# Conditioning products of a two-layer diffusion step: their four partial strips go over DRAM and are added by VectorE instead of by a selector matmul

## The chip, the cores and the metric

The kernel runs on one core of one Trainium2 chip. The core has TensorE (PE; its weight loads are shown apart as PEld), VectorE (DVE), ScalarE (ACT), GpSimd (POOL) and SyncE (SP), which here only issues DMAs, and 16 DMA engines. The metric is the device time of one execution in microseconds: the median was 1292.72 us over three runs (1290.27 to 1293.17).

## What is computed

A batch of 256 context tokens and 1024 latent tokens, each a row of 1024 numbers, goes through two layers. Cut to what matters here, with l = 0 the gated linear attention (GLA) and l = 1 the softmax attention:

```python
for l in range(2):
    mod_p = silu(c_ctx) @ w_ada[l] + b_ada[l]      # context tokens, one vector of 3072
    mod_s = silu(c) @ w_ada[l] + b_ada[l]          # latent tokens
    sh, sc, gt = split(mod, 3)                     # shift, scale, gate: 1024 each
    h = rms_norm(x, norm_g[l]) * (1 + sc) + sh
    out = gla_mixer(h) if l == 0 else attention(h)
    x = x + gt * out
```

So there are four conditioning vectors in all, two conditionings by two layers. The shift and scale of layer 0 are needed before any token can be projected; its gate only at layer 0's output projection. The shift and scale of layer 1 are needed when the first finished tile of layer 0 is normalised again, its gate only at the last projection. The weights `w_ada` are 2 x 12 MB, and the products are tiny: two vectors by a matrix.

## The kernel before, in words

All large products are made as three f16 products of a high and a low part, and before each split into parts a weight is scaled by a power of two. `pow2` finds it: VectorE reduces the largest absolute value of each partition, one small matmul against the identity (line 113) spreads the 128 values over a PSUM bank, VectorE reduces that (line 118) and makes the scale in four tiny steps. The bank is named by `p2_bank`: in set-up and in GLA it is "z", a single buffer, which also takes half of the transposes of the tokens in set-up (line 420; the other half take the two "mm" banks).

Set-up loads four tiles of tokens, the first query and key weights and layer 0's shift and scale weights (eight loads of 1 MB), makes silu of the conditioning vectors (`cond_vectors`), normalises and transposes the tokens, splits the weights (`fill`, `split_rank`), and then multiplies the conditioning (`mod_rows`, line 294). Those products are ordered on TensorE behind the maxima of the weights. Then `affine` makes layer 0's scaled shift and scale, and `modulate` applies them to the transposed tokens, with which the first projections (line 557) begin.

The GLA is a loop over 50 slots, one head and one tile of 128 tokens each: four heads by ten tiles for the first scan direction, and each head's second direction one head later. In a slot come the decays, the chunk's own products, the value and gate projections for the next slot (`value_gate`), the scans, and a `filler` that brings in other work: in odd slots up to 31 the load of a block of 256 columns of `w_ada` (`ada_load`; layer 0's four gate blocks first, then layer 1's twelve), in even slots the products of the block loaded before (`gemv`), in the slot after it their sum (`mod_sum`). Other jobs, appended to a list, run in the next slot: splits of the attention weights that go to DRAM for later, output weights, and at slots 34 and 35 layer 1's `affine` and the transposition of its result to rows (`affine_rows`).

`gemv` packs eight small products into four strips of 32 partitions, so that the result in the PSUM bank "mm" is four partial sums, of which two rows in each strip are of use. ScalarE copies it to the tile "mod" (one buffer). `mod_sum` adds the strips with a selector matrix `k.sel` (a one in row 32j+i, column i): for a shift or scale block two matmuls with the copied product as weights (line 335) give the sums transposed, and VectorE adds the bias (line 337); for a gate block one matmul with the selector as weights (line 345) gives rows, VectorE adds the bias loaded for it (lines 344 and 346), and SP stores the rows to `gt_d` in DRAM (line 347). These gate rows use the single buffer "s0" of the scan's start states.

The gate projection's result is copied to the tile "gx" (line 589, two buffers), goes through silu and is multiplied with the normalised scan output (line 748), from where SP stores it (line 749, `og_d<-gx`).

The order of the instructions on each engine is not the order of the code. A planner of the framework simulates the program with modelled times and lets each engine take, of what is ready, what has the best priority; priority follows the order of the code, shifted by the offsets of the table `LATER` for the named blocks (`with self.later(...)`). `issue_after` adds a fixed order on one engine. SP, like each engine, works off its queue in order: a DMA that waits holds up those behind it. A tile of a pool with one buffer is given to its next user when all that read it are done.

Of the kernel before, what the change touches and what calls it, by code (L numbers as in the profile page):

```python
# [17 lines left out]
P = 128  # L18
# [54 lines left out]
class K:  # L73
# [57 lines left out]
    def mulcol(self, a, b, pool, tag, const=None):  # L131
        o = self.t(pool, [P, 1], F32, tag)
# [53 lines left out]
    def fill_out(self, w, st):  # L186
# [13 lines left out]
        so = self.t(self.small, [P, 2], F32, "wso")  # L200
# [69 lines left out]
    def cond_vectors(self, rows, brow):  # L270
        nc, cp = self.nc, self.const
        ps = self.bank("z")
        nc.tensor.transpose(ps[:, 0:32], rows, self.ident[0:32, 0:32])
        nc.tensor.transpose(ps[:, 32:80], brow, self.ident[0:48, 0:48])
        cT = self.t(cp, [P, 80], F32, "cT")
        nc.vector.tensor_copy(cT, ps[:, 0:80])
        self.gT = cT[:, 16:32]
        self.bT = cT[:, 32:80]
        c = self.t(cp, [P, 16], F32, "silu_c")
# [4 lines left out]
        nc.vector.tensor_copy(self.cst[:, :, 0:2], c.rearrange("p (i k) -> p k i", i=2))  # L284
        self.modT = [self.t(cp, [P, 16, 2], F32, f"modT{l}") for l in range(2)]

    def mod_rows(self, rows):
# [12 lines left out]
        for b in range(4):  # L302
            nc.tensor.transpose(ps[:, b * P : b * P + P], m[:, b * P : b * P + P], self.ident)
        nc.vector.tensor_tensor(
            self.modT[0].rearrange("p (j b) i -> p j b i", j=4),
            ps.rearrange("p (b j r) -> p j b r", b=4, j=4)[:, :, :, 0:2],
            self.bT[:, 0:16].rearrange("p (j b) -> p j b", j=4).unsqueeze(3).to_broadcast([P, 4, 4, 2]), ALU.add,
# [7 lines left out]
    def gemv(self, l, b, to):  # L315
# [10 lines left out]
        return l, b, m  # L326


    def mod_sum(self, l, b, m):
        nc = self.nc  # L330
        ps = self.bank("mm")
        if b < 8:
            for j in range(2):
                o = 2 * j
                nc.tensor.matmul(ps[:, o : o + 2], m[:, j * P : j * P + P], self.sel[:, 0:2], start=True, stop=True)
            f = 2 * b
            nc.vector.tensor_tensor(
                self.modT[l][:, f : f + 2, :], ps[:, 0:4].rearrange("p (f i) -> p f i", i=2),
                self.bT[:, 24 * l + f : 24 * l + f + 2].unsqueeze(2).to_broadcast([P, 2, 2]), ALU.add,
            )  # L340
        else:
            a = 256 * (b - 8)
            r = self.t(self.ew, [P, DV], F32, "s0", bufs=1)[0:2, :]
            nc.sync.dma_start(r, self.I["b_ada"][l : l + 1, 2 * D + a : 2 * D + a + 256].to_broadcast([2, 256]))
            nc.tensor.matmul(ps[0:2, 0:256], self.sel[:, 0:2], m, start=True, stop=True)
            nc.vector.tensor_tensor(r, ps[0:2, 0:256], r, ALU.add)  # L346
            nc.sync.dma_start(self.gt_d[l, :, a : a + 256], r)


    def affine(self, l):  # L350
        nc, sp = self.nc, self.const
        mod = self.modT[l]
        gb = self.t(sp, [P, 2, 2, KT], F32, f"gb{l}")
        g, sh = (gb[:, j].rearrange("p i k -> p k i") for j in range(2))
        gT = self.gT[:, 8 * l : 8 * l + 8].unsqueeze(2).to_broadcast([P, KT, 2])
        nc.vector.scalar_tensor_tensor(g, mod[:, 8:16, :], 1.0, gT, ALU.add, ALU.mult)
        m = self.t(self.small, [P, 2], F32, "wmx")
        for j, t in enumerate((mod[:, 0:8, :], g)):
            nc.vector.tensor_reduce(m[:, j : j + 1], t, AX.XY, ALU.max, apply_absolute_value=True)
        mx = self.t(self.small, [P, 1], F32, "af_m", bufs=1)  # L360
        nc.vector.scalar_tensor_tensor(mx, m[:, 1:2], 32.0, m[:, 0:1], ALU.mult, ALU.add)
        s, inv = self.pow2(mx)
        nc.vector.tensor_scalar(sh, mod[:, 0:8, :], s, None, ALU.mult)
        nc.vector.tensor_scalar(g, g, s, None, ALU.mult)
        c = self.t(sp, [P, 1], F32, f"invh{l}")
        nc.vector.tensor_copy(c, inv)
        return gb, g, sh, c


    def affine_rows(self, gb):  # L370
        ps = self.bank("mm")[0:32, 0:P]
        self.nc.tensor.transpose(ps, gb.rearrange("p s i k -> p (s i k)"), self.ident)
        r = self.t(self.ew, [P, 256], F32, "mod", bufs=1)[0:32, 0:P]
        self.nc.vector.tensor_copy(r, ps)
        self.nc.sync.dma_start(self.gb_d.rearrange("s i (k p) -> (s i k) p", p=P), r)
# [30 lines left out]
    def normalise(self, xs, junk):  # L406
        nc = self.nc
        n = len(xs)
        ssq = self.t(self.sm, [P, n], F32, f"nt_s{n}")
# [79 lines left out]
    def rank_scales(self):  # L489
        nc, inv = self.nc, self.inv_rank  # L490
        inv_r = self.mulcol(self.inv_h, inv[:, 0:1], self.small, "inv_r")
# [3 lines left out]
        one = self.t(self.small, [P, 2], F32, "one")  # L495
# [4 lines left out]
        row = self.mulcol(one[:, 0:1], self.sr, self.small, "one_r")  # L500
        ones = self.r[96:98, :]
        nc.vector.tensor_scalar(ones, ones, row[96:98, :], None, ALU.mult)
        t = self.mulcol(inv_r, one[:, 1:2], self.small, "inv_z")
# [74 lines left out]
    def value_gate(self, h, i, w):  # L578
# [8 lines left out]
        if h > 0:  # L587
            x = self.t(self.ew, [P, DV], F32, "gx")
# [335 lines left out]
    def gla_out(self, wo, early, n0):  # L924
# [3 lines left out]
        self.inv_h = self.mod1[3]  # L928
# [14 lines left out]
        for n in range(n0, NT):  # L943
            i = order[n]
            if n == NT - 1:
                self.query_rest()
                with self.tc.issue_after(self.pe):
                    self.query()
                self.key_tile(order[n - 2], wkv)
                self.query_rest()  # L950
            hT, lT, inv = prep.pop(i)
            x = xs.pop(n)
            last = self.residual(i, lambda k: (hT[:, k, :], lT[:, k, :]), wo, inv, x)
            nc.gpsimd.dma_start(self.x1_d[i], x)
            self.last = last
            with self.tc.issue_after(last):
                if n + 2 in rows:
                    prep[order[n + 2]] = self.out_prep(*rows.pop(n + 2))
# [6 lines left out]
            self.mod_tile(i, x, (t[:, 0], t[:, 1]), self.last)  # L965
            for j in {3: (0,), 4: (1, 2), 5: (3,), 6: (4,), 7: (5,), 8: (6,)}.get(n, ()):
                self.key_tile(order[j], wkv)
            if n == 8:
                with self.tc.issue_after(self.pe):
                    self.query()  # L970
            if n == n0:
# [9 lines left out]
                with self.tc.issue_after(last):  # L981
                    self.att_setup(*ckv)
                    self.key_setup(*ckv, inv)
# [298 lines left out]
    def attention(self, wo, wk):  # L1282
# [7 lines left out]
        for n, (p, c) in enumerate(self.steps):  # L1290
# [8 lines left out]
            for e in range(4):  # L1299
                h = 4 * p + e  # L1300
                if later:
                    self.nc.sync.dma_start(*later.pop(0))
                PT = self.t(self.sp, [P, 20, 256], F16, "PT", bufs=3)
                self.scores(h, c, 0, q[(p, c, 0)], PT)
                if e % 2 == 0:
                    self.query()
                    self.rest()
                    self.scores(h, c, 1, q[(p, c, 1)], PT)
                else:
                    self.query_rest()  # L1310
                if len(pend) == 2:
                    self.values(*pend[0], g.pop(pend.pop(0)[0]))
                else:
                    self.key_tile(len(pend), wkv)
                if e % 2 == 1:
                    self.scores(h, c, 1, q[(p, c, 1)], PT)
                pend.append((h, c, PT))
                if e % 2 == 1:
                    g.update({i: self.gateT(i, c, *wg[p]) for i in (h - 1, h)})
                    self.rest()  # L1320
# [9 lines left out]
        self.out_tile(OUT[0], 0, self.t(self.sp, [P, TS + PAST], F32, "p")[:, 0:D], wo)  # L1330
        for t in pend:
            self.values(*t, g.pop(t[0]))
# [50 lines left out]
def emit(ctx, tc, I, O, dbg=None, stop=None):  # L1383
# [15 lines left out]
    k.gt_d = k.t(k.dram, [2, 2, D], F32, "gt_d")  # L1399
    k.gb_d = k.t(k.dram, [2, 2, D], F32, "gb_d")  # L1400
# [6 lines left out]
    k.sel = k.t(k.const, [P, 2], F32, "sel")  # L1407
# [5 lines left out]
    with ExitStack() as c:  # L1413
# [5 lines left out]
        k.p2_bank = "z"  # L1419
        banks = ("z", "cs", "A", "kt", "U", "o")  # L1420
        k.gla_init()
        with ExitStack() as c1:
# [3 lines left out]
            rows = k.t(k.p1, [32, P], F32, "rows")  # L1426
            brow = k.t(k.p1, [48, P], F32, "brow")
# [3 lines left out]
            small(rows[16:32, :], I["norm_g"].rearrange("l (k p) -> (l k) p", p=P))  # L1431
# [267 lines left out]
```

## Time and profile before

| | before |
|---|---|
| median of three runs | 1292.72 us |
| profiled execution, own time | 1293.64 us |
| its span | 1291.9 us |
| TensorE busy | 1209.2 us, 94% |
| VectorE busy | 920.0 us, 71% |
| ScalarE busy | 706.0 us, 55% |
| granted TensorE clock, mean | 0.991 |

The span is that of one execution as the profiler saw it; its own time is 1.7 us longer. Rows of groups give a line, an engine, an operation, the tile written and those read, the shapes, a count, and times in nanoseconds. Rows of the time line give the start and the length in microseconds; in brackets the idle time before, and what ended it. Matmuls overlap: the next one starts before the last one has ended. An f32 matmul shows as two records. The stages are roughly these: set-up to 85 us, GLA to 560 us, the output projection of layer 0 with the keys and values of layer 1 to 700 us, attention to 1190 us, the last projection to the end.

### The profile page before, as it was taken

Reading aid. Unit: us, or ns where it says so; the run is one execution under the profiler, and the core shown is the slowest. Engines: PE = TensorE matmul, PEld = TensorE weight load, DVE = VectorE, ACT = ScalarE, POOL = GpSimd, SP = SyncE. Lnnn points to the kernel's source line nnn. Section 1 sums busy time; section 2 is a strip of 40 time slices with the busy share of each in tenths; the row PEclk is TensorE's granted clock in tenths of the full one; section 3 lists DMA queues with packets and bytes.
Section 4 is the critical chain, followed back from the end, with each engine's and each line's share of the span. In section 5 each row is a group of like instructions: output and inputs, shape, how many; then the busy total and the mean of one; then the engine's idle time right before and its main releaser. Section 6 shows DMA issues by size and latency. Waiting matters only on the chain. (4 is left out here: it accounts for less than half of the span.)

```text
span 1291.9 us, 22221 instructions
## 1 busy us (share of the span) xinstructions
PE 1209.2 (94%) x7936; PEld 778.7 (60%) x7936; DVE 920.0 (71%) x2120; ACT 706.0 (55%) x1706; POOL 353.3 (27%) x594
## 2 busy tenths in 40 slices
PE   3899999999999989897999889999999999989998
PEld 1367666655555546664776557676666767656444
DVE  4676678877778789767676667677767677785552
ACT  2684466756656656642334376666767686673110
POOL 1132113223321243410223334342243345312000
PEclk9999999999999999998999999999999999999999
DMA  9711566455555543459965696667957657879432
GB/s 358 259 34 34 164 199 202 149 166 159 160 158 177 172 127 107 147 138 329 210 143 156 176 200 121 136 135 131 198 116 164 136 106 145 185 138 228 139 143 82
DMA packets 357454, 207.51 MB, mean 161 GB/s; under 512 B 251054, under 2 KB 341438, under 8 KB 354912
## 3 DMA queue, kind: packets, MB, share of 16 engines
q1 hardware_dynamic: 349824, 188.02, 57.1%
q0 software_dynamic: 4080, 12.73, 3.0%
q10 hardware_dynamic: 3440, 5.35, 1.1%
q8 instruction: 62, 1.02, 0.3%
q14 instruction: 48, 0.39, 0.1%
HBM read 107.45 MB, written 37.26 MB: 112 GB/s over the span
## 5 line engine op out<-in xcount | busy, mean ns | idle before, releaser
L155 PEld LDWEIGHTS <-hT_hi 128*128 128x128 f16 x1920 | 188.8, 99 | 124.2 <-issue 12.4
L155 PE MATMUL mm<-whi,hT_hi 128*128 128x512 f16 (+1 forms) x576 | 201.1, 349 | 2.9 <-ACT gx L589 1.8
L155 PE MATMUL mm<-whi,hT_lo 128*128 128x512 f16 (+1 forms) x576 | 200.8, 349 | 0.2 <-DMA hT_lo<-hl 0.2
L155 PE MATMUL mm<-wlo,hT_hi 128*128 128x512 f16 (+1 forms) x560 | 195.0, 348 | 0.0
L1214 DVE SCALAR_TENSOR_TENSOR phl<-p,srec,phl 128x1280 f16<-128x1280 f32 (+1 forms) x80 | 107.6, 1347 | 72.4 <-POOL phl L1211 37.9
L155 PEld LDWEIGHTS <-whi 128*128 128x128 f16 x1232 | 120.1, 98 | 60.8 <-issue 2.4
L155 PE MATMUL mm<-hT_hi,whi 128*128 128x256 f16 (+1 forms) x480 | 141.0, 294 | 0.7 <-DVE s L346 0.7
L155 PE MATMUL mm<-hT_hi,wlo 128*128 128x256 f16 (+1 forms) x480 | 141.0, 294 | 0.0
L155 PE MATMUL mm<-hT_lo,whi 128*128 128x256 f16 (+1 forms) x480 | 141.0, 294 | 0.0
L155 PEld LDWEIGHTS <-hT_lo 128*128 128x128 f16 x960 | 94.5, 98 | 70.0 <-DMA hT_lo<-k 5.4
L1181 PE MATMUL S<-kT,wst 128*128 128x512 f16 (+1 forms) x624 | 122.9, 340 | 12.7 <-ACT p L1189 12.2
L155 PE MATMUL mm<-PT,vh 128*128 128x256 f16 x672 | 112.2, 273 | 9.8 <-DMA PT<-phl 8.0
L1211 POOL TENSOR_SCALAR phl<-p,srec 128x1280 f16<-128x1280 f32 (+1 forms) x40 | 57.2, 1430 | 192.1 <-DVE srec L1205 83.1
L1184 DVE TENSOR_REDUCE smx<-S 128x1 f32<-128x1280 f32 (+1 forms) x80 | 101.5, 1269 | 9.2 <-PE S L1181 9.0
L1189 ACT ACTIVATE p<-S,snb,sexp 128x1280 f32<-128x1280 f32 (+1 forms) x80 | 99.4, 1242 | 5.3 <-DVE phl L1214 1.8
L1181 PEld LDWEIGHTS <-wst 128*128 128x128 f16 x624 | 61.1, 98 | 65.7 <-issue 14.5
L155 PE MATMUL mm<-PT,vl 128*128 128x256 f16 x336 | 91.6, 273 | 0.0
L155 PEld LDWEIGHTS <-wlo 128*128 128x128 f16 x616 | 60.3, 98 | 31.5 <-DVE wlo L1352 1.8
L155 PEld LDWEIGHTS <-vh 128*128 128x128 f16 x672 | 65.1, 98 | 20.7 <-issue 9.4
L1019 POOL TENSOR_TENSOR rope<-hx,ropet 128x64 f32<-128x64 f32 x160 | 63.1, 424 | 32.2 <-ACT hx L1145 16.7
L178 DVE TENSOR_REDUCE wmx<-wst 128x1 f32<-128x512 f32 x104 | 65.0, 676 | 5.9 <-DMA wst<-in_att_w_in 2.5
L1186 ACT ACTIVATE snb<-smx,nsexp 128x1 f32<-128x1 f32 x80 | 23.3, 291 | 75.3 <-DVE smx L1184 73.4
(370 smaller groups left out, 2694.5 us busy)
## 6 DMA issues: line engine op xcount, KB each, us to landing
wada<-in_w_ada SPq DMA_DIRECT2D x16, 1024.0 KB, 5.2
wst<-in_gla_w_in SPq DMA_DIRECT2D x12, 1024.0 KB, 5.0
wst<-in_att_w_in SPq DMA_DIRECT2D x10, 1024.0 KB, 5.5
og_d<-gx SPq DMA_DIRECT2D x40, 128.0 KB, 2.7
og_d<-og POOLq DMA_DIRECT2D x40, 128.0 KB, 3.0
wst<-og_d SPq DMA_DIRECT2D x5, 1024.0 KB
xr<-x_d SPq DMA_DIRECT2D x9, 512.0 KB, 6.4
out<-xr ACTq DMA_DIRECT2D x17, 256.0 KB, 3.0
```

What stands on the lines that cost most here:

```text
L155: self.pe = self.nc.tensor.matmul(out, a, b, start=k == 0 and j == 0, stop=k == n - 1 and j == 2).ins
L178: nc.vector.tensor_reduce(mx[:, j : j + 1], st[:, 2 * j : 2 * j + 2, :], AX.XY, ALU.max, apply_absolute_value=True)
L1019: nc.gpsimd.tensor_tensor(tv[:, h, :, w, :], xv[:, h, :, 1 - w, :], sn[:, :, w, :], ALU.mult)
L1181: nc.tensor.matmul(S[:, a : a + n], x, y, start=m == 0, stop=m == 2)
L1184: last = nc.vector.tensor_reduce(mx, S, AX.X, ALU.max).ins
L1186: nc.scalar.activation(nb, mx, AF.Copy, scale=self.nsexp)
L1189: nc.scalar.activation(p, S, AF.Exp, scale=self.sexp, bias=nb, accum_out=den)
L1211: nc.gpsimd.tensor_scalar(hi, p, r, 2.0 ** 14, ALU.mult, ALU.mult)
L1214: nc.vector.scalar_tensor_tensor(lo, p, r2, hi, ALU.mult, ALU.subtract)
```

## The change

Layer 0's shift and scale are made as before. The other sixteen blocks keep their products and the copy to "mod", but the copy is now stored to a new DRAM tensor `md_d` of 128 rows by 3072 columns for each layer. `mod_load` brings back what is wanted in a layout with 8 neighbouring columns in each of the 128 partitions, the four strips side by side (runs of 32 bytes): once in slot 9 for layer 0's gate, once in slot 34 for all of layer 1. It reads into the "mod" buffer. A job in slot 11 (`gate_rows`) and one in slot 36 (`mod_rows_out`) add the strips with reductions on VectorE, add the bias, and store the gate to `gt_d`; the second also makes layer 1's scaled shift and scale and stores them to `gb_d` directly in the order of rows. The selector, the second layer's transposed biases and norm weights, `affine_rows` and its transposing matmul are gone. `affine` is split: `fit` is its part common to both layers.

In set-up, `p2_bank` is "o" instead of "z" (again "z" from the end of set-up). The tile "gx" of the GLA has three buffers. Tiles of single columns in the pool "small", and the sums of squares in `normalise`, are given fewer buffers. Many calls in the attention layer and in its approach are wrapped in `later` with new names, for which the table has no entry, so that their offset is 0.

```diff
-    def cond_vectors(self, rows, brow):
+    def cond_vectors(self, rows):
...
-        nc.tensor.transpose(ps[:, 0:32], rows, self.ident[0:32, 0:32])
-        nc.tensor.transpose(ps[:, 32:80], brow, self.ident[0:48, 0:48])
+        nc.tensor.transpose(ps[:, 0:40], rows, self.ident[0:40, 0:40])
...
     def gemv(self, l, b, to):
...
         m = self.t(self.ew, [P, 256], F32, "mod", bufs=1)
         nc.scalar.copy(m, ps[:, 0:256])
-        return l, b, m
-    def mod_sum(self, l, b, m):
...
-                nc.tensor.matmul(ps[:, o : o + 2], m[:, j * P : j * P + P], self.sel[:, 0:2], start=True, stop=True)
...
-            r = self.t(self.ew, [P, DV], F32, "s0", bufs=1)[0:2, :]
-            nc.sync.dma_start(r, self.I["b_ada"][l : l + 1, 2 * D + a : 2 * D + a + 256].to_broadcast([2, 256]))
-            nc.tensor.matmul(ps[0:2, 0:256], self.sel[:, 0:2], m, start=True, stop=True)
-            nc.vector.tensor_tensor(r, ps[0:2, 0:256], r, ALU.add)
-            nc.sync.dma_start(self.gt_d[l, :, a : a + 256], r)
+        nc.sync.dma_start(self.md_d[l, :, 256 * b : 256 * b + 256], m)
+
+    def mod_load(self, l, s, n):
+        t = self.t(self.ew, [P, 256], F32, "mod", bufs=1)
+        md = t[:, 0 : 64 * n].rearrange("p (s j i k) -> p s j i k", s=n, j=4, i=2)
+        bias = t[:, 192 : 192 + 8 * n].rearrange("p (s k) -> p s k", s=n)
+        src = self.md_d[l].rearrange("(j r) (s p k) -> s r p j k", r=32, s=3, k=KT)
+        load = self.nc.sync.dma_start
+        for m in range(n):
+            for i in range(2):
+                load(md[:, m, :, i], src[s + m, i])
+        load(bias, self.I["b_ada"][l].rearrange("(s p k) -> p s k", s=3, k=KT)[:, s : s + n])
+        if n == 3:
+            load(t[:, 216:224], self.I["norm_g"][l].rearrange("(p k) -> p k", k=KT))
+        return l, md, bias, t[:, 216:224]
+
+    def mod_sum(self, md, bias, tag):
+        nc = self.nc
+        n = md.shape[1]
+        m = self.t(self.const, [P, n, 2, KT], F32, tag)
+        for a in range(n):
+            nc.vector.tensor_reduce(m[:, a], md[:, a].rearrange("p j i k -> p i k j"), AX.X, ALU.add)
+        nc.vector.tensor_tensor(m, m, bias.unsqueeze(2).to_broadcast([P, n, 2, KT]), ALU.add)
+        return m
+
+    def gate_store(self, l, m):
+        self.nc.sync.dma_start(self.gt_d[l].rearrange("i (p k) -> p i k", k=KT), m)
+
+    def gate_rows(self, l, md, bias, _):
+        self.gate_store(l, self.mod_sum(md, bias, "gm")[:, 0])
+
+    def mod_rows_out(self, l, md, bias, gn):
+        m = self.mod_sum(md, bias, "mod1")
+        self.gate_store(l, m[:, 2])
+        gb = self.t(self.const, [P, 2, 2, KT], F32, "gb1")
+        c = self.t(self.const, [P, 1], F32, "invh1")
+        s, inv = self.fit(m[:, 0], m[:, 1], gb[:, 0], gn.unsqueeze(1).to_broadcast([P, 2, KT]))
+        self.nc.vector.tensor_scalar(gb[:, 1], m[:, 0], s, None, ALU.mult)
+        self.nc.vector.tensor_scalar(gb[:, 0], gb[:, 0], s, None, ALU.mult)
+        self.nc.vector.tensor_copy(c, inv)
+        for j in range(2):
+            self.nc.sync.dma_start(self.gb_d[j].rearrange("i (p k) -> p i k", k=KT), gb[:, j])
+        self.inv_h1 = c
+
+    def fit(self, sh, sc, g, gn):
+        nc, sp = self.nc, self.small
+        nc.vector.scalar_tensor_tensor(g, sc, 1.0, gn, ALU.add, ALU.mult)
+        m = self.t(sp, [P, 2], F32, "wmx")
+        for j, t in enumerate((sh, g)):
+            nc.vector.tensor_reduce(m[:, j : j + 1], t, AX.XY, ALU.max, apply_absolute_value=True)
+        mx = self.t(sp, [P, 1], F32, "af_m", bufs=1)
+        nc.vector.scalar_tensor_tensor(mx, m[:, 1:2], 32.0, m[:, 0:1], ALU.mult, ALU.add)
+        return self.pow2(mx)
...
-    def affine_rows(self, gb):
-        ps = self.bank("mm")[0:32, 0:P]
-        self.nc.tensor.transpose(ps, gb.rearrange("p s i k -> p (s i k)"), self.ident)
...
-            x = self.t(self.ew, [P, DV], F32, "gx")
+            x = self.t(self.ew, [P, DV], F32, "gx", bufs=3)
...
-        k.p2_bank = "z"
+        k.p2_bank = "o"
...
+        k.p2_bank = "z"
         k.tl = k.pool("tl", ctx=c)
...
         def filler(slot):
             if slot < 4:
                 prompt(slot)
-            if part:
-                k.mod_sum(*part.pop())
+            if slot in (9, 34):
+                gm.append(k.mod_load(*((0, 2, 1) if slot == 9 else (1, 0, 3))))
+            if slot in (10, 35):
+                k.jobs.append(((k.gate_rows if slot == 10 else k.mod_rows_out), *gm.pop()))
             if slot % 2 == 0:
                 if held:
-                    part.append(k.gemv(*held.pop()))
+                    k.gemv(*held.pop())
...
-            if slot == 34:
-                k.jobs.append((lambda: setattr(k, "mod1", k.affine(1)),))
-            if slot == 35:
-                k.jobs.append((k.affine_rows, k.mod1[0]))
...
             if n == NT - 1:
-                self.query_rest()
+                with self.later("x.qr"):
+                    self.query_rest()
...
```

More of the change, by code (lines that the diff above doesn't have):

```diff
@@ L284, in cond_vectors @@
         nc.vector.tensor_copy(self.cst[:, :, 0:2], c.rearrange("p (i k) -> p k i", i=2))
-        self.modT = [self.t(cp, [P, 16, 2], F32, f"modT{l}") for l in range(2)]
+        self.modT = self.t(cp, [P, 16, 2], F32, "modT")
     def mod_rows(self, rows):
@@ L957, in gla_out @@
                 if n + 2 in rows:
-                    prep[order[n + 2]] = self.out_prep(*rows.pop(n + 2))
+                    with self.later("x.prep"):
+                        prep[order[n + 2]] = self.out_prep(*rows.pop(n + 2))
             load(n + 2)
@@ L1633, in _constants @@
     f32 = np.float32
-    sel = np.zeros((P, 2), f32)
-    for j in range(4):
-        for i in range(2):
-            sel[32 * j + i, i] = 1
     half = P // 2
```

148 lines of the change are left out of this document (73 added, 75 removed).

## The prediction

> **What bounds the kernel now.** First the page: its span and engine rows, and the PE row of the 40 slices.
>
> ```profile
> span 1291.9 us, 22221 instructions
> PE 1209.2 (94%) x7936; PEld 778.7 (60%) x7936; DVE 920.0 (71%) x2120; ACT 706.0 (55%) x1706; POOL 353.3 (27%) x594
> PE   3899999999999989897999889999999999989998
> ```
>
> TensorE is busy 94% of the span; the low digits are the first slice (set-up) and the middle. The view of busy time by stretch shows where TensorE has no slack (columns: stretch, PE busy, PEld, DVE, ACT, POOL, clock, DMA share, GB/s).
>
> ```profile
> 107.00:450.00 343.00, 341.65 (x2094) 202.58 (x2092) 263.97 (x714) 200.97 (x517) 86.51 (x155) 1.00 0.53 163
> 450.00:500.00 50.00, 44.10 (x225) 25.96 (x218) 44.58 (x131) 29.30 (x85) 21.19 (x34) 0.94 0.36 108
> 500.00:550.00 50.00, 44.58 (x301) 32.17 (x300) 38.36 (x108) 33.33 (x88) 19.40 (x32) 0.99 0.44 141
> 550.00:600.00 50.00, 45.09 (x315) 30.84 (x313) 32.20 (x79) 17.23 (x35) 7.09 (x13) 0.97 0.78 208
> 600.00:650.00 50.00, 45.59 (x356) 35.11 (x354) 39.23 (x90) 17.85 (x40) 10.54 (x22) 0.97 0.99 234
> ```
>
> From 107 to 450 us TensorE is busy 341.65 of 343 us, VectorE only 263.97. The conditioning products run exactly there, in the odd jobs of slots 2 to 33. A microsecond of TensorE work removed in this stretch is a microsecond of the span, unless VectorE takes over. From 450 to 650 TensorE idles 200 − (44.10 + 44.58 + 45.09 + 45.59) = 20.6 us: there waits decide.
>
> **1. The sums leave TensorE.** The rows of the selector tile and of the copies into the strips, the selector's busy time in the stretch, and four starts on the time line:
>
> ```profile
> L335 PE MATMUL mm<-sel,mod x32: 167/251/251, 201.9 to 367.9; 128*128 128x2 f32 x32
> L345 PE MATMUL mm<-mod,sel x16: 377/378/378, 119.2 to 461.3; 128*2 128x256 f32 x16
> L325 ACT COPY mod<-mm x16: 351/368/389, 110.0 to 452.1; 128x256 f32<-128x256 f32 x16
> 107.00:450.00 343.00, 8.23 (x46) 5.36 (x46) 1.00 0.53 163
> 119.16 0.59 PE L345 MATMUL mm<-mod,sel 128*2 128x256 f32 x2
> 119.69 0.23 PE L629 MATMUL cs<-cum,ghi 128*128 128x130 f16 x1
> 201.91 0.50 PE L335 MATMUL mm<-sel,mod 128*128 128x2 f32 x4
> 202.28 0.68 PE L676 MATMUL U<-v,ks 128*128 128x256 f32 x2
> ```
>
> Four L335 records make one sum of a shift or scale block, two L345 records one of a gate block: eight sums of each kind. Busy time overlaps its neighbours, so I price by starts: 119.69 − 119.16 = 0.53 and 202.28 − 201.91 = 0.37 us. 8 × 0.53 + 8 × 0.37 = 7.2 us; the busy 8.23 us is the other bound. I take −7.2, because the next instruction's start is what moves. The layer-1 transpose of the scaled rows (L372) goes too, in the stretch with idle time: nothing. The 16 products stay, and each still needs its "mm" bank and its copy L325.
>
> **2. The way over DRAM, on the queues.** SP loses 8 bias loads and 8 gate stores and one store of rows; it gains 16 strip stores, 2 strip loads and a bias load with one store (gate of layer 0), and 6 strip loads, bias, norm weight and three stores (layer 1): 31 issues for 17.
>
> ```profile
> L347 SPq DMA_DIRECT2D gt_d<-s x8: 250/264/317, 123.2 to 467.1; - x8
> SPq L347 <- DVE s L346: 22.1, 5, 12.8
> q1 hardware_dynamic: 77324, 62.18, 50.0%
> ```
>
> 14 more issues at 0.26 to 0.32 us are 4 us of a queue that mostly waits, spread over 400 us: nothing. Each strip store makes SP wait for its ScalarE copy; queued behind are the gated-row stores and the weight loads. The old gate stores made SP wait 22.1 us in five cases for the sum, and VectorE never showed it. I take nothing, with +2 as the upper end. The layer-1 loads are 6 × 512 + 384 + 128 = 3,584 pieces of 32 B. From 107 to 512 us, 77,324 packets took 50.0% of 16 engines' 405 us, 42 ns each; 3,584 × 42 / 16 = 9.4 us, an estimate and an upper one, as those packets average 0.8 KB. Their reader runs as a job of slot 36, the loads go out in slot 34; slots last (452.1 − 110.0) / 30 = 11.4 us by the L325 row. The cover is at least one slot, so nothing; with the cover gone VectorE would stand for up to 9.4 us. The Trainium skill, page "DMA: Bandwidth & Descriptors" (Specifications), speaks against this part: it has transfers below 512 B do a read-modify-write, and asks for 512 B or more at line rate. No row here has a load of 32 B pieces, so the trace can't settle it; it is rival D below.
>
> **3. VectorE takes the sums.**
>
> ```profile
> L346 DVE TENSOR_TENSOR s<-mm,s x8: 402/405/412, 122.7 to 466.6; 2x256 f32<-2x256 f32 x8
> L359 DVE TENSOR_REDUCE wmx<-modT x2: 156/160/163, 43.7 to 482.8; 128x1 f32<-128x16 f32 x2
> L473 DVE TENSOR_REDUCE wmx<-wada x1: 406/406/406, 25.2 to 25.2; 128x1 f32<-128x256 f32 x1
> ```
>
> Eight adds of 0.405 us (3.2 us) and eight small adds go, four reductions over 64 elements come, between 0.16 and 0.41 us each by the two reductions shown, and two small adds. VectorE comes out some 2 us lighter, but off the path up to 450 us: nothing. Around 490 us, where it is busy 44.58 of 50, three of the reductions come together ahead of layer 1's maximum: up to +1, as the copy of the transposed rows goes there. I take 0.
>
> **4. The wait it adds.** The strips are read into the single "mod" buffer in slot 9; the reduction that frees it is a job of slot 11; the product of slot 10 wants the same buffer for its copy. So that product sits in one of the two "mm" banks until the job has run, up to one slot (11.4 us). Behind it TensorE has the value and gate projections, which then have one bank and must wait for ScalarE's copies, two per slot. The nearest row for such a wait is TensorE on the gate copy, in part 6: 1.8 us in four cases, about 0.45 each. Two to eight such waits: +1 to +4. I take +1: it happens once, the product is late in its slot.
>
> **5. Set-up's maxima in bank "o".** Rows of PE, VectorE and ScalarE on the time line:
>
> ```profile
> 29.33 1.11 PE L420 MATMUL z<-ident,x 128*128 128x128 f32 x4 [0.79 <-DVE xT L1458]
> 31.23 0.27 PE L113 MATMUL z<-ident,wm 128*128 128x128 bf16 x1 [0.78 <-DVE xT L1458]
> 32.83 1.94 PE L294 MATMUL A<-whi,cst 128*32 128x512 f32 x8
> 40.07 1.89 PE L294 MATMUL A<-hT_lo,cst 128*32 128x512 f32 x16
> 25.49 1.21 DVE L474 TENSOR_REDUCE wmx<-wada 98x1 f32<-98x1024 f32 x1
> 27.50 0.17 DVE L284 COPY cst<-silu_c 128x16 f32<-128x16 f32 x1
> 28.59 0.69 DVE L1458 COPY xT<-z 128x512 f32<-128x512 f32 x1 [0.91 <-PE z L420]
> 30.49 0.69 DVE L1458 COPY xT<-z 128x512 f32<-128x512 f32 x1 [1.21 <-PE z L420]
> 31.53 0.29 DVE L118 TENSOR_REDUCE p2m<-z 128x1 f32<-128x128 f32 x1 [0.35 <-PE z L113]
> 39.55 1.28 DVE L484 SCALAR_TENSOR_TENSOR wa<-wada,p2s,wa 34x1024 f16<-34x1024 f32 x1
> 40.87 1.14 ACT L485 ACTIVATE wa<-wada,p2s 1x1024 f16<-1x1024 f32 x1 [1.86 <-DVE wa L484]
> 42.04 0.37 ACT L299 COPY mod<-A 128x256 f32<-128x256 f32 x1
> ```
>
> The first maximum (L113) queues for bank "z" behind the last transpose, though its weights are ready much earlier; the layer-0 products (L294) are ordered behind the third maximum and run 32.83 to 41.96. With a bank of their own the maxima need only L474 (done 26.70), and the products also L284 (27.67): they could start 5.2 us earlier. But VectorE is nearly full: it ends at 40.83 (L484) and can only reclaim its 0.91 + 1.21 + 0.35 = 2.5 us of idle time. ScalarE's L485 follows L484, and the copy L299, on which the modulation of all tokens hangs, follows L485. So I take −2.5; the ends are −4.9 (the planner puts L299 ahead of L485) and 0 (the full DMA queue delays the last weight rows). Dropping one constant load and two bias rows: nothing, they land before the first transposes need VectorE.
>
> **6. A third gate buffer.** The waits view, 500 to 650 us, and one line from the gate tile's view (ScalarE's idle time, by what ended it):
>
> ```profile
> PE mm L155 <- ACT gx L589: 1.8, 4, 0.6
> PE o L736 <- POOL Sc L701: 1.6, 1, 1.6
> PE z L736 <- POOL Sc L701: 1.4, 1, 1.4
> PE y L155 <- DMA hT_lo<-k: 4.9, 1, 4.9
> PE kv L113 <- DVE amx L1076: 4.1, 1, 4.1
>   DMA og_d<-gx: 6.0, 7
> ```
>
> ScalarE waits 6.0 us for gated rows to leave, and TensorE 1.8 us for ScalarE. I take −1.5 of the 1.8; the upper end adds the 3.0 us of scan waits that a gate projection run ahead could fill: −4.8; the lower end is 0.
>
> **The rest of the edits.** Fewer buffers for one-off columns and sums of squares: the cover is that each is used once or twice; nothing. The named priority blocks have no entry in the offsets table: offset 0, nothing.
>
> **Sum.** −7.2 + 0 + 0 + 1 − 2.5 − 1.5 = −10.2. The profiled execution took 1293.64 us, 0.92 above the median of the runs; 1293.64 − 10.2 − 0.92 = 1282.5 us. With the bounds of the parts alone, 1275 to 1290.
>
> **The rivals.**
> A, the bounds all fall well: −8.2 − 4.9 − 4.8 = −17.9, 1275 us. For it: no row excludes them. Against: three ends at once.
> B, VectorE takes over as pace-maker: it is at 44.58 of 50 us after 450 us and would have to be above TensorE for long stretches before. Only then is half of the 7.2 lost, and with the bank hold (+4) and set-up at 0 the result is 1292.7 − 3.6 − 1.5 + 4 = 1291.6. Against: 263.97 of 343.
> C, slower: the order on the engines is written by a planner from modelled times, and removing 16 sums and adding DRAM round trips makes it write another one for 450 to 650 us, where TensorE's idle 20.6 us are a few long waits (4.9 and 4.1 above): in order, it stands wherever a modelled time was too short. Doubled, they cost 20.6: 1303. It cancels the gain from +10.2, and ends slower from +12.8. For it: such waits exist already. Against: they could as well shrink.
> D, the strips come late: the 32 B pieces cost so much more than 42 ns that the reader on VectorE stands before layer 1's modulation. At twice the estimate, 18.8 us, against one slot of 11.4, VectorE loses 7.4 and TensorE after it: 1290. Its rule is the one named in part 2.
>
> **How the numbers follow.** Main case 0.52 (1283, own range 1277 to 1289); A 0.16; B 0.10; C 0.16; D 0.06. Range 1273 to 1296: below A by 2 for the planner's luck, and into C. 0.2% is 2.6 us, about what a measurement of this kernel can tell: faster means below 1290.1. That holds for the main case, A, and a third of B and D, 0.73; the same 0.10; slower is C and a little of B, 0.17.
>
> **What would show it.** No selector rows on PE, and the products, values and gates of slots 2 to 33 about 7 us shorter at an equally full PE; L294's first row near 28 to 30 us and the first projection (L557) 2 to 3 us ahead of before; TensorE's wait on the gate copies near 0; one held bank around slot 10; VectorE not standing on a DMA before layer 1's shifts and scales. It is wrong if PE's idle time between 450 and 650 us grows by over 10 us, if PE is no longer full up to 450, or if the attention stage, which the edits don't touch, moves by several microseconds.

## The result and the profile after

The changed kernel takes 1285.75 us (1278.49 to 1288.88), before in the same comparison 1292.99 us: a ratio of 0.9933, 95% interval 0.9909 to 0.9958. Two further comparisons gave 0.9906 [0.9886, 0.9927] and 0.9914 [0.9895, 0.9933]. It is faster by 7 to 12 us; forecast were 10.2. The sum came out nearly right, but two of its terms did not: what was booked to the sums on TensorE comes only in the company of the third gate buffer, which was booked at 1.5 us. That the total is near has luck in it.

The page of the changed kernel, span and engines, and the granted clock in 40 slices (the profiled execution took 1285.86 us):

```profile
span 1284.1 us, 22149 instructions
...
PE 1199.3 (93%) x7886; PEld 777.7 (61%) x7886; DVE 916.8 (71%) x2109; ACT 703.1 (55%) x1706; POOL 351.0 (27%) x594
...
PEclk9999999999999999988999999999999999999999
```

50 matmul records fewer, TensorE's busy time 9.9 us lower, VectorE's 3.2. The stretches, with the columns of the prediction's view:

```profile
104.00:439.00 335.00, 332.63 (x2059) 200.56 (x2057) 264.68 (x706) 201.48 (x521) 85.57 (x156) 1.00 0.56 174
...
450.00:650.00 200.00, 181.12 (x1244) 129.61 (x1243) 155.24 (x404) 95.20 (x240) 56.38 (x97) 0.95 0.70 181
```

104 to 439 us is the stretch of the products now. TensorE is still full (332.63 of 335) and VectorE far from it. From 450 to 650 TensorE idles 18.9 us (20.6 before), at a mean clock of 0.95. Set-up, on the time line:

```profile
27.99 1.94 PE L292 MATMUL A<-whi,cst 128*32 128x512 f32 x8
...
38.25 1.06 PE L292 MATMUL A<-hT_lo,cst 128*32 128x512 f32 x8 [1.57 <-DMA hT_lo<-in_w_ada]
...
40.74 0.19 DVE L302 TENSOR_TENSOR modT<-cs,cT 128x32 f32<-128x32 f32 x1 [0.53 <-PE cs L301]
```

The products start at 27.99 instead of 32.83 us, but at 38.25 they stand 1.57 us on a DMA: the last weight rows. The first projection (L569 now) is 2.7 us ahead of before. The strip loads, by their source line:

```profile
L334 SPq DMA_DIRECT2D mod<-md_d x8: 359/500/1861, 177.8 to 449.5; - x8
...
DMA to landing us min/median/max: 2.0/3.9/4.7
```

and the reductions of layer 1 by theirs:

```profile
L345 DVE TENSOR_REDUCE mod<-mod x3: 242/242/246, 479.4 to 479.7; 128x16 f32<-128x64 f32 x3
```

The loads in pieces of 32 bytes land 2.0 to 4.7 us after their issue, against a cover of one slot (11.4 us). Three reductions run at 479.4 us, some 25 us behind their loads. And what TensorE waits for between 440 and 640 us (us in total, times, longest):

```profile
PE kv L113 <- DVE amx L1099: 8.9, 1, 8.9
PE y L155 <- DMA hT_hi<-q: 4.7, 1, 4.7
PE z L748 <- POOL Sc L713: 3.3, 1, 3.3
PE o L748 <- POOL Sc L711: 2.2, 1, 2.2
PE mm L155 <- ACT gx L601: 1.1, 1, 1.1
```

The wait on the gate copies is down from 1.8 to 1.1 us, and the wait for the attention's maxima, `amx`, has grown from 4.1 to 8.9.

**Where the lead comes and goes.** The lead is the start of an instruction before less its start in the changed kernel. It is 2.8 us at the first product copy and 13.1 at the last one, 16.8 at the last product of the scan with its state (537 us before, `o<-Sc,qe`), 19.8 at the first product of layer 0's output (574 us), 15.3 at the first query copy (703 us), 18.0 at 889, 11.4 at 1113, and 8.0 at the end. So TensorE's lead grows to some 20 us, against 10.2 forecast, and more than half of that is lost again. ScalarE's gate copy at 538 us is 26.7 us ahead, but a copy with a third buffer may start sooner without TensorE being sooner. The experiments ask where the lead comes from and who takes it.

### The profile page after: what moved, and what is told of

Read it like the earlier page. It is cut to its first block, busy times and chain, and to the rows that moved or that the text cites. A ratio compares the mean times of both kernels' runs of the same rounds, so it can differ in the third digit from the quotient of the medians.

```text
span 1284.1 us, 22149 instructions
## 1 busy us (share of the span) xinstructions
PE 1199.3 (93%) x7886; PEld 777.7 (61%) x7886; DVE 916.8 (71%) x2109; ACT 703.1 (55%) x1706; POOL 351.0 (27%) x594
## 5 line engine op out<-in xcount | busy, mean ns | idle before, releaser
L1204 PE MATMUL S<-kT,wst 128*128 128x512 f16 (+1 forms) x624 | 122.5, 338 | 12.6 <-ACT p L1212 11.8
```

Of the source, the lines that this page charges most:

```text
L1204: nc.tensor.matmul(S[:, a : a + n], x, y, start=m == 0, stop=m == 2)
```

## The experiments

Theory 1 is the prediction's: a microsecond taken from TensorE in the full stretch is a microsecond of the time, and the parts add up. Theory 2: behind 450 us TensorE stands on waits, and what was gained before is given back there.

**Each part alone.** `e_sums` is the changed kernel with the other two parts undone:

```diff
-            x = self.t(self.ew, [P, DV], F32, "gx", bufs=3)
+            x = self.t(self.ew, [P, DV], F32, "gx")
...
-        k.p2_bank = "o"
+        k.p2_bank = "z"
```

> Only the strips over DRAM, summed by VectorE; maxima in bank z, two gate buffers. Theory 1 (each microsecond of TensorE work taken out of the full stretch is a microsecond of the time): set-up as before, first product copy at 110.0 us; the copies draw ahead slot by slot, the last one at 444 to 446 us (452.1 before), and the total is 5 to 8 us shorter. Theory 2 (the order is written anew and the stalls after 450 us and the half-clock windows that follow them decide): the last product copy is early as by theory 1, but the total lies anywhere from 15 us shorter to 5 longer, with the difference made between 500 and 620 us or in half-clock windows.

`e_bank` is before with "o" for the maxima of set-up, and "z" again ahead of the loop over the slots:

```diff
-        k.p2_bank = "z"
+        k.p2_bank = "o"
...
+        k.p2_bank = "z"
```

> Only the set-up's maxima in bank o. Theory 1: first projection at 44.8 us (47.4 before), first product copy near 107.3, last one near 449.5, total 2 to 3 us shorter. Theory 2: the same 2.6 us up to 110 us, then the total moves by up to 5 us either way, at the stalls after 450 us.

`e_gx` is before with the third buffer and with the smaller column tiles that make room for it:

```diff
...
-            x = self.t(self.ew, [P, DV], F32, "gx")
+            x = self.t(self.ew, [P, DV], F32, "gx", bufs=3)
```

> Only the third gate buffer, with the smaller column buffers that make room for it. Theory 1: no change up to 450 us (copies at 110.0 and 452 us), the wait of TensorE for gate copies between 500 and 560 us falls from 1.8 to under 0.5 us, total 0 to 2 us shorter. Theory 2: the gate projections run ahead through the last ten slots and free more than that, 5 to 10 us by 560 us, of which the output stage gives part back.

`e_again` is the changed kernel itself:

> The changed kernel again, for a second profile. Theory 1: 1283 to 1288 us, the same waits in the same places, the lead over before 13 us at the last product copy, 15 at the first score product, 8 at the end. Theory 2: the places of the instructions are the same, but the half-clock windows fall elsewhere, and with them several of the 18.7 - 10.4 = 8.3 us of lost clock by which its first profile is worse than that of before.

Measured: sums alone 1.0007 [0.9988, 1.0025], bank alone 0.9962 [0.9947, 0.9977], third buffer alone 0.9982 [0.9967, 0.9997], all of it 0.9906. The three ratios multiply to 0.9951; the parts do not add up. Above all, the part with most of the forecast gain brings none alone, though its TensorE is 10.7 us ahead at the last product copy.

**Two parts at a time, and the sums gone without a substitute.** `e_nogx` is the changed kernel with the first edit of `e_sums` only:

> The changed kernel with two gate buffers again: sums and bank without the third buffer. Theory 1 (the parts add up): sums alone measured 1.0007 and the bank alone 0.9962, so 0.997, some 1289 us, and the third buffer is worth what it was alone, 2.3 us in ratio 0.9982. Theory 2 (what is gained before 540 us is given back in the output stage of layer 0, where the DMA queues set the pace, by how the waits fall): the sum of the parts does not hold; anything from 0.993 to 1.000, and TensorE's lead over before at the first score product (10 us or more at 452 us) says how much came through.

`e_bankgx` is before with the edits of `e_bank` and `e_gx`:

> Before with the maxima in bank o and the third gate buffer, the sums still on TensorE. Theory 1: 0.9962 x 0.9982 = 0.9944, some 1286 us; then the sums bring only 0.1 to 0.4 per cent in company. Theory 2: the third buffer's lead is given back at 600 to 620 us as it was when it stood alone, and 0.996 is left, the bank's part, which went through when alone.

`e_nosum` is before without the sums:

```diff
-        ps = self.bank("mm")
+        ps = m
...
-                nc.tensor.matmul(ps[:, o : o + 2], m[:, j * P : j * P + P], self.sel[:, 0:2], start=True, stop=True)
...
-            nc.tensor.matmul(ps[0:2, 0:256], self.sel[:, 0:2], m, start=True, stop=True)
```

> Before with the 48 selector matmuls of the 16 sums left out and nothing put in their place: VectorE adds the bias to the unsummed product, so the conditioning rows of all sums are wrong and the output with them. No strips go over DRAM. Theory 1: TensorE 7.2 to 10 us ahead at 452 us and the same at the end: 0.992 to 0.9945. Theory 2: 7 to 10 us ahead at 452 us, at most 3 us of it left at 700 us, ratio 0.998 to 1.001. If the loss of some 6 us at 955 to 1030 us in the changed kernel comes from the added DMA issues, it is absent here; if it comes from TensorE being ahead, it is here too.

`e_sumsgx` is the changed kernel with `p2_bank` back to "z", and `e_again2` the changed kernel beside it:

> The changed kernel with the set-up's maxima back in bank z: sums and third buffer. Theory 1 (the parts add up): 1.0007 x 0.9982 = 0.9989. Theory 3 (the third buffer is what lets the sums' gain through: with TensorE ahead, ScalarE's gate copies come too late for two buffers): TensorE 20 us or more ahead at 540 us as in the changed kernel, ratio 0.993 to 0.996, only the set-up's 2.6 us or a little more short of the whole change.

> The changed kernel once more, beside the runs below: 0.9906 to 0.9933 as measured before, some 1283 to 1286 us.

All eight combinations, with the ratio to before, the lead in us at four instructions (named by their time before; the last scan product is TensorE's, the copies are ScalarE's), and ScalarE's idle time ahead of the gate copies that ends with the store of an earlier tile's rows, `og_d<-gx`:

| kernel | ratio, 95% interval | last product copy, 452 | gate copy, 538 | last scan product, 537 | first query copy, 703 | ScalarE on `og_d<-gx` |
|---|---|---|---|---|---|---|
| before | 1 | 0 | 0 | 0 | 0 | 6.0 us |
| third buffer | 0.9982 [0.9967, 0.9997] | 0.0 | 4.3 | -2.4 | -0.8 | 1.4 us |
| bank | 0.9962 [0.9947, 0.9977] | 3.6 | 6.0 | 6.2 | 6.5 | 4.9 us |
| bank, third buffer | 0.9988 [0.9971, 1.0004] | 3.2 | 9.1 | 2.4 | 3.8 | 1.4 us |
| sums | 1.0007 [0.9988, 1.0025] | 10.7 | 11.0 | 11.0 | 4.8 | 20.1 us |
| sums, bank | 0.9999 [0.9981, 1.0017] | 12.6 | 13.9 | 14.0 | 5.3 | 23.5 us |
| sums, third buffer | 0.9931 [0.9918, 0.9944] | 11.5 | 25.0 | 16.3 | 13.0 | 4.1 us |
| all | 0.9914 [0.9895, 0.9933] | 14.9 | 27.9 | 18.9 | 18.5 | 4.0 us |

(The rows of the first column name the parts that are in; the last one is `e_again2`. The leads come from one profiled execution each; those of "bank, third buffer" and "all" were the fastest of theirs, 4 and 6 us below the median, so the ratios are the firmer column.) Read the rows with the sums in pairs. TensorE is 11 to 15 us ahead at the last product copy in all four. At the last scan product it is 11 and 14 us ahead with two gate buffers, 16 and 19 with three. The gate copy at 538 us overstates this: with the third buffer alone it starts 4.3 us earlier while TensorE is 2.4 us behind.

With the sums gone the third buffer is worth 0.76% (1.0007 to 0.9931, 9.8 us), and 0.85% with the bank as well. With the sums in place it is worth 0.18%, and with the bank as well it costs 0.26% (0.9962 to 0.9988; `e_bankgx` lies above what either theory gave). The other way round, the sums gone are worth 0.51 and 0.74% where the third buffer is in (6.6 and 9.6 us), and nothing or a loss where it is not. Each of these differences is uncertain by some 3 us. That is Theory 3 of the expectation. Its mechanism begins in the view of the tile gx (ScalarE's idle time by what ended it), here of `e_sums`:

```profile
  DMA og_d<-gx: 20.1, 9
  PE mm L155: 16.0, 24
```

and of the changed kernel:

```profile
  PE mm L155: 21.4, 26
  ACT ls L258: 5.4, 8
  POOL ors L146: 4.2, 8
  DMA og_d<-gx: 4.1, 3
```

Before, the same line had 6.0 us. With TensorE ahead and two buffers it is 20.1 us in nine waits, during which ScalarE does nothing else.

How TensorE comes to pay for it shows in a stretch that `e_sums` and `e_sumsgx` run with the same 268 matmuls in the same order. First the busy times in `e_sums`, then in `e_sumsgx`, then what ScalarE waits for in `e_sums` from 443 to 500 us:

```profile
442.67:498.00 55.33, 52.89 (x268) 31.57 (x268) 46.18 (x132) 30.67 (x87) 19.50 (x34) 0.97 0.43 124
```

```profile
441.53:492.86 51.33, 51.33 (x268) 31.95 (x269) 46.41 (x134) 32.07 (x93) 19.26 (x34) 0.97 0.47 140
```

```profile
ACT gx L601 <- DMA og_d<-gx: 8.5, 2, 5.3
```

`e_sums` needs 55.33 us and `e_sumsgx` 51.33. In `e_sums` ScalarE stands 8.5 us on the stores of earlier rows, in `e_sumsgx` it never does, and TensorE has six short waits of 0.3 to 0.5 us for results of ScalarE and VectorE that `e_sumsgx` has not. They are 2.4 of the 4.0 us; the rest are starts that come late while the matmul before still runs. `e_nogx` and `e_again2` differ by 4.3 us in the same stretch. So some 4 of the 9.8 us are shown as the price of the missing buffer. The rest is not traced to it: from 499 us on the planner gives TensorE another order in some 38 places, and no run holds the order and changes only the buffer.

TensorE's waits in `e_sums`, 440 to 650 us:

```profile
PE y L155 <- DMA hT_hi<-oghl: 12.8, 1, 12.8
PE mm L155 <- ACT gx L601: 4.4, 2, 3.5
PE o L748 <- POOL Sc L711: 2.6, 1, 2.6
PE kv L113 <- DVE amx L1099: 2.2, 1, 2.2
```

and in `e_sumsgx`, 440 to 640 us:

```profile
PE kv L113 <- DVE amx L1099: 9.5, 1, 9.5
PE y L155 <- DMA hT_hi<-q: 5.0, 1, 5.0
...
PE mm L155 <- ACT gx L601: 1.9, 2, 1.4
```

The wait on the gate copies went from 1.8 us before to 4.4, and with the third buffer to 1.9. The long wait of 12.8 us in the output stage is not what the third buffer removes: `e_sumsgx` stands 9.5 and 5.0 us in the same place, where `e_sums` stands 12.8 and 2.2.

`e_nosum` takes 1.0039 [1.0021, 1.0058]: with the work of the sums gone and nothing added, the kernel is slower, which neither theory gave. So the way over DRAM and VectorE's reductions are not what eats the gain in `e_sums` (1.0007); work taken from TensorE alone is worth nothing here. ScalarE stands 12.7 us on `og_d<-gx` in it, but TensorE only 0.4 us on a gate copy; whether a third buffer would bring its gain through was not run. It is 7.8 us ahead at the last product copy, 0.8 at 703 us, 5.7 behind at 1113.

**More work in the same place.** `e_dblsum` doubles the selector matmuls of before; those of the gate blocks are shown:

```diff
...
-            nc.tensor.matmul(ps[0:2, 0:256], self.sel[:, 0:2], m, start=True, stop=True)
+            for _ in range(2):
+                nc.tensor.matmul(ps[0:2, 0:256], self.sel[:, 0:2], m, start=True, stop=True)
```

> Before with every selector matmul of the 16 sums done twice (the second writes the same values over the first). Theory 1 (a microsecond of TensorE work in the full stretch is a microsecond of the time): 7 to 10 us behind at 452 us and at the end, 1.0055 to 1.008. Theory 2 (the output stage of layer 0 is paced by its queues and VectorE): 7 to 10 us behind at 452 us, most of it made up by shorter waits of TensorE between 540 and 650 us, ratio 1.000 to 1.003.

Measured 1.0130 [1.0105, 1.0155], 16 us: more than either theory gave. Its profiled execution, at 1319.44 us, is the slowest of six and 9 us above their median, so the losses read from it are on the large side. TensorE is 9.7 us further behind at the last product copy than at the first projection, as Theory 1 has it, but nothing of it is made up later, and 5.5 us more are lost by 703 us and 4.8 in the attention. Theory 2 in its simple form, a stage with a pace of its own that absorbs a lead and a delay alike, is refuted. Taking work out and putting work in both add waits or half-clock windows behind 450 us.

**Can the output stage of layer 0 be relieved?** `e_dma` moves two loads of 1 MB later, by a small copy into the tile that must come first:

```diff
+            if n == n0:
+                nc.vector.tensor_copy(self.ropet[:, 0, 0, 0:1], x[:, 0:1])
+                nc.sync.dma_start(self.ropet, self.I["k_rope"])
-            if n == 4:
+            if n == 5:
                 self.q0 = self.t(self.wp, [P, KT, 512], F16, "whi2")
+                nc.vector.tensor_copy(self.q0[:, 0, 0:1], x[:, 0:1])
                 nc.sync.dma_start(self.q0, self.ahead["q0"][0][:, 0])
...
-        nc.sync.dma_start(self.ropet, I["k_rope"])
```

> The changed kernel with two loads of 1 MB each moved later, the table of the rotary angles and the first part of the query weights, which went out at 573 and 588 us into a full queue: they now wait for a tile that the third and the sixth residual leave. Theory 2 (the output stage is paced by the DMA queues): the transposes at 575 to 594 us no longer take 9.4 and 4.3 us to issue, TensorE's idle time from 450 to 650 us falls from 18.9 to under 14 us, and the time falls by 3 to 7 us against the changed kernel, to 0.988 to 0.991 of before. Theory 1 (only TensorE's work counts, and its idle time there has other causes): no change, 0.9906 to 0.9933.

`e_dmalate` has that and the set-up of the attention one residual later:

```diff
+            if n == n0 + 1:
+                with self.tc.issue_after(last):
+                    with self.later("x.setup"):
+                        self.att_setup(*ckv)
+                    with self.later("x.kset"):
+                        self.key_setup(*ckv, kinv)
...
-                with self.tc.issue_after(last):
-                    with self.later("x.setup"):
-                        self.att_setup(*ckv)
-                    with self.later("x.kset"):
-                        self.key_setup(*ckv, inv)
```

> The changed kernel with the two 1 MB loads moved later as in the run before, and the attention's set-up (the maxima of the cached keys and values, whose cross-partition step made TensorE wait 8.9 us) put behind the fourth residual instead of the third. Theory 2: the waits of TensorE on these maxima and on the next tile's transposes between 575 and 595 us, 8.9 us in the changed kernel and 6.2 us with the loads alone moved, fall under 3 us, and 3 to 6 us of it stay to the end: 0.985 to 0.989. If instead the stage's pace is set by the bytes alone, the wait moves to the next tile and the time stays at 0.990.

Measured 0.9900 [0.9879, 0.9922] and 0.9915 [0.9893, 0.9938], both within the intervals of the two further comparisons of the changed kernel. TensorE's waits, 440 to 650 us, in `e_dma` and then in `e_dmalate`:

```profile
PE y L155 <- DMA hT_hi<-oghl: 6.2, 1, 6.2
PE y L155 <- DMA hT_hi<-q: 5.1, 1, 5.1
PE z L748 <- POOL Sc L713: 3.3, 1, 3.3
```

```profile
PE y L155 <- DMA hT_hi<-oghl: 4.8, 1, 4.8
PE y L155 <- DMA hT_hi<-q: 4.3, 1, 4.3
PE z L748 <- POOL Sc L713: 3.3, 1, 3.3
```

The wait of 8.9 us on `amx` is gone from the list, and one of 6.2 or 4.8 us for the next tile's transposes has taken its place: the wait moves on. The ratio of `e_dma` lies in the range of its Theory 2, but not by that theory's way: from 450 to 650 us TensorE idles 18.5 us, where under 14 were expected and the changed kernel has 18.9. No version beats the changed kernel beyond the intervals. What sets the pace from 560 to 600 us is left open; the two loads moved in `e_dma` are not it.

## Why the prediction was right, and where it was not

**The sums leave TensorE (-7.2).** The size was a little low: the lead grows by 10.3 us over the 16 blocks in the changed kernel (13.1 less 2.8), by 10.4 in `e_sums`, by 8.0 in `e_nosum`, and falls by 9.7 in `e_dblsum`; that is 0.5 to 0.65 us a sum against the 0.37 and 0.53 read from starts. The step that failed is the sentence behind it, "A microsecond of TensorE work removed in this stretch is a microsecond of the span, unless VectorE takes over". It is one at 452 us, with VectorE far from full. At the end it is 1.0007 alone; where the third buffer is in, the sums are worth 6.6 and 9.6 us, about the 7.2 booked. I named VectorE as the only thing that could take the gain back. Instead ScalarE, waiting for a buffer, made TensorE wait for its results (4.0 us are shown so), and the output stage and the attention took more: in `e_sums` the lead of 10.7 us is 4.8 at 703 us, 5.3 at 889 and -1.4 at 1113.

**A third gate buffer (-1.5, ends -4.8 and 0).** Mis-sized by a factor of more than six: -2.3 us alone, but -9.8 us (1.0007 to 0.9931) with the sums gone. The row I priced it from, 6.0 us of ScalarE on `og_d<-gx` and 1.8 us of TensorE on ScalarE, was right for before and belonged to a TensorE that is not ahead. In `e_sums` the same rows have 20.1 and 4.4 us. Two edits of one change were priced apart from the same profile, although the first moves the engine that the second one's row depends on. The total came near because the two terms err in opposite ways: without the buffer, booked at 1.5 us, the other edits, booked at 8.7 us, bring a ratio of 0.9999 (`e_nogx`).

**Set-up's maxima (-2.5, ends -4.9 and 0).** The lead at the first projection is 2.3 to 3.2 us in `e_bank`, `e_bankgx`, `e_nogx` and the changed kernel. The products start 4.8 us earlier, and the reason named for the end 0 takes part of it, a DMA that is late with weight rows (1.57 us at 38.25). Alone the part gave 0.9962, 4.9 us, of which 3.3 are there at the first product copy; with sums and third buffer it goes from 0.9931 to 0.9914, with the third buffer only from 0.9982 to 0.9988, both inside the intervals. The end -4.9 stands in the prediction without its working; the start that it names is 5.2 us earlier.

**The wait it adds (+1).** It is there, and in slot 10, in the changed kernel's rows of PE, VectorE and ScalarE:

```profile
187.10 1.07 PE L318 MATMUL mm<-wada,cst 128*32 128x256 f32 x16
...
191.01 0.25 DVE L345 TENSOR_REDUCE gm<-mod 128x16 f32<-128x64 f32 x1
...
194.08 0.17 DVE L346 TENSOR_TENSOR gm<-gm,mod 128x16 f32<-128x16 f32 x1
...
194.27 0.37 ACT L323 COPY mod<-mm 128x256 f32<-128x256 f32 x1 [2.12 <-DVE gm L346]
```

The product's bank is held from 188.2 to 194.3 us. TensorE had other work: from 150 to 200 us it is busy 49.16 of 50, so the hold cost at most 0.84.

**The way over DRAM, VectorE's share (0 and 0).** Right, as far as the runs tell: `e_sums`, which has both, is not slower than `e_nosum`, which has neither. Rival D is refuted by the strip loads' 4.7 us at most. The Trainium skill's page "DMA: Bandwidth & Descriptors" (Specifications) has transfers below 512 B do a read-modify-write; for eight loads of 16 KB in 32 B pieces no run here shows a price. The upper bound 1290 of the sum leaves out the upper ends +2 and +1 of these parts; with them it is 1292.5.

**Rivals A, B and C.** A needed 17.9 us. B is out: VectorE 264.68 of 335. C, more idle time behind 450 us, is what happened in `e_sums`, `e_nogx` and `e_nosum`: by 703 us it had taken 6 to 7 us of the lead, and the attention took the rest or more. In the changed kernel idle time from 450 to 650 us fell to 18.9. The order that the planner writes, C's own ground, differs between all these kernels and stays untested by itself.

**A sign of error that came true.** The prediction called itself wrong if the attention stage, which the edits don't touch, moved by several microseconds. It did: from 889 to 1113 us the lead falls by 6.6 us in the changed kernel, by 4.6 to 7.6 in every other kernel with fewer or more matmuls for the sums (4.8 in `e_dblsum`), and by 0.9 at most in `e_bank`, `e_gx` and `e_bankgx`, though before and the changed kernel have the instructions of this stage in the same order. Added DMA issues are not the cause (`e_nosum` adds none), nor is being ahead (`e_bankgx` is 8.7 us ahead). What the fall is made of can be read: between these two points TensorE idles 8.6 us in the changed kernel and 6.4 before, and loses 3.4 us to half clock against none, 5.6 of the 6.6 us. In all ten kernels and repeats with changed sums half clock costs 1.7 to 3.4 us here, in before, `e_bank`, `e_gx` and `e_bankgx` nothing. Why the waits are longer is open; how a wait of two microseconds becomes nearly four is shown below.

Closing the sum over the whole span, from all matmul rows and the clock record: before, 1291.9 = 1199.3 of work at full clock + 82.7 idle + 9.9 lost at half clock. After, 1284.1 = 1184.6 + 84.8 + 14.8; `e_sums`, 1294.2 = 1182.8 + 93.5 + 17.9. Work fell by 15 to 17 us, more than the selector rows' 8.23, which I can't fully assign; in `e_sums` idle time and clock took back 18.8.

## What to carry to other kernels

Work taken from the busiest engine only moves that engine forward; price the waits behind it again for an engine that is that much earlier, first of all the tiles with two buffers whose writer already waits a few microseconds for their reader. A lead is read on the engine that it is about: a copy with one more buffer moves by itself. Edits of one change that touch the same chain are priced together, or one of them alone looks worthless and the other one cheap. And a lead counts where the last stage starts, not where the full stretch ends.

## What the runs showed of the hardware

I had not expected what a wait of two microseconds on TensorE costs. The time line of the changed kernel in the attention:

```profile
919.23 0.27 PE L155 MATMUL mm<-PT,vl 128*128 128x256 f16 x1
919.34 0.49 PE L1204 MATMUL S<-kT,wst 128*128 128x256 f16 x3
921.92 0.49 PE L1204 MATMUL S<-kT,wst 128*128 128x256 f16 x3 [2.09 <-ACT p L1212]
922.49 0.58 PE L155 MATMUL mm<-PT,vh 128*128 128x256 f16 x2
922.87 0.42 PE L155 MATMUL mm<-PT,vl 128*128 128x256 f16 x1
```

The same place before, where the wait is 1.14 us:

```profile
938.01 0.82 PE L1181 MATMUL S<-kT,wst 128*128 128x256 f16 x6
939.96 0.39 PE L155 MATMUL mm<-PT,vh 128*128 128x256 f16 x2 [1.14 <-DMA PT<-phl]
940.19 0.27 PE L155 MATMUL mm<-PT,vl 128*128 128x256 f16 x1
```

After 2.09 us the same matmul takes 0.42 instead of 0.27 us, and matmuls start at half the rate, until the record of the clock that TensorE was granted goes back to full (925.6 us). The record is made of windows of 3.413 us, each at 1.0 or 0.5. Over all 14 profiled runs, between 60 and 1270 us, 72 windows at full clock had TensorE busy for less than 40%, and the next window was at half clock in all 72; of 32 with 40 to 48% it was so in 10, of 4,724 with more in 2. A half-clock window with full work costs 1.7 us. So by these figures a wait of some 2.1 us, 60% of a window, costs 3.8 if it falls into one window, and 2.1 if a window's border halves it (an estimate). The page "TensorE: Matmul & The Clock Gate" (Part 1) of the Trainium skill has these free-running windows of 3.4 us, and sets the gap to avoid at more than 3.4 us; the runs here show two microseconds to be enough. The prediction priced every wait at its own length; in the profiled executions the changed kernel lost 14.8 us to the clock and before 9.9.
